# A hybrid encoder step: three PSUM banks for the scores instead of two, two for the dense products instead of three, and dense operands on multiples of 512 bytes

## The chip, the cores and the metric

One core of one Trainium2 chip runs the whole program. The metric is the device time of that core in microseconds (us). The kernel before took 2956.35 us, the median of three runs (2955.74 to 2959.2).

## The reference

One layer of a streaming encoder, on 2,128 token columns in one pass (64 of a running stream, 16 meta tokens, 2,048 of a new stream), model width 1,024:

```
h = rms_norm(x);  p = h @ w_in                       # 1024 -> attention, RG-LRU and GLA columns
o_att = rms_norm(softmax(q0 k0)v - lam*softmax(q1 k1)v)   # 4 heads, block-causal chunks of 64
o_lru = rg_lru(causal_dwconv(lx)) * gelu(lg)
o_gla = rms_norm(gla_blocked(gq, gk, gv, log_g)) * silu(gog)
x = x + concat(o_att, o_lru, o_gla) @ w_out
h = rms_norm(x)
x = x + (gelu(causal_dwconv3(h @ ffn_w_up)) * (h @ ffn_w_gate)) @ ffn_w_down   # 1024 -> 2816 -> 1024
y = rms_norm(x)
```

It also returns the new K and V rows and the end states of the recurrences and convolutions.

## The kernel before

**Precision.** Every dense product is three matmuls in fp32r: each operand is split into a high part and a rest (`whi`, `wlo` for weights; `hh`, `hl`, `h2h`, `h2l`, `gh`, `gl` for activations), and high x high, rest x high and high x rest are summed in one PSUM bank. A weight tile is 128 columns wide and is the stationary operand; the activations are the moving operand, up to 512 columns. So every matmul brings a weight load (the engine PEld) with it.

**Streams.** `Flow.run` takes steps in turn from three generators: `dense` (the input projection `win`, then the FFN of groups of tokens), `attention` (scores and values) and `recurrent` (RG-LRU and GLA). The order in which instructions stand on each engine is then made by the framework's scheduler from these streams' priorities and from the buffers that are free, so a different number of buffers gives another order everywhere.

**Stages.** The input projection (lines 641 and 643, tile `ps_w`) runs to some 800 us. Then come three groups of tokens, `FGROUPS = [[512], [512], [336, 256, 512]]`. For each, `wout` multiplies by w_out (L1434, tile `pd`), `up_gate` makes for each of 22 slices of the FFN one product `pu` and one `pg` per block of tokens (L1299, 24 matmuls each), and `down` adds them into the residual (L1366, tile `pd`, added to x by VectorE at L1372). Groups 1 and 2 run beside attention and recurrences, to about 2020 us. Group 3 (1,104 tokens) runs alone after it, with pools of its own opened in `open3`.

**Eviction.** A product leaves its bank in different ways. `pu` is copied out by ScalarE (L1316). `pg` is read by VectorE (L1334), and only after the convolution and GELU of `pu` (L1316 to L1329, ScalarE and VectorE in turn) are done. A score tile `ps_sc` (L1052, perhaps a mask at L1057, and L1059) is read twice: by VectorE for the row minimum `NB` (L1061) and then by ScalarE for the exponential `pc` (L1062).

**PSUM.** It has eight banks. Before: three for the dense products (`ps_w`, which up to 2020 us also serves `pd`), two for scores (`ps_s`), one each for transposes, values and recurrences. In group 3 the last five are given to `pd` (`ps_x`), while `pu` and `pg` keep `ps_w`.

**SBUF.** Pools are laid one behind the other from the left, and others from the right end. The small constants (`cst`) come first, then the weight buffers `wp` (two `raw`, three `whi`, three `wlo`, 4 KB per partition each), then the pools of the stage. From the tiles' sizes, the weight buffers began 32 bytes past a multiple of 512, and so did the activations of the projection and of groups 1 and 2. In group 3 the activations `h2h`, `h2l` began 480 bytes past one, and `gh`, `gl` (1,104 columns, with blocks at columns 0, 336 and 592) began at changing places.

Of the kernel before, what the change touches and what calls it, by code (L numbers as in the profile page):

```python
# [10 lines left out]
F32 = mybir.dt.float32  # L11
# [7 lines left out]
PSUM = bass.MemoryType.PSUM  # L19
DRAM = bass.MemoryType.DRAM  # L20

P = 128
# [41 lines left out]
FGROUPS = [[512], [512], [336, 256, 512]]  # L64
# [71 lines left out]
def tile_hymba_step(ctx, tc, xT, xkT, cache_v, wi, wo, wu, wg, wd, par, sgla, c_msk, yT_p, yT_s, nkT_p, nv_p, lh_p, lc_p, gs_p, fc_p,  # L136
                    nkT_s, nv_s, lh_s, lc_s, gs_s, fc_s):
    nc = tc.nc
# [20 lines left out]
    env = {}  # L159
# [12 lines left out]
    NPC, NRC, NW, NRAW, NSQ = 9, 9, 3, 2, 3  # L172
    cst = ctx.enter_context(tc.tile_pool(name="cst", bufs=1))
    wp = ctx.enter_context(tc.tile_pool(name="wp", bufs=1))
    ps_w = ctx.enter_context(tc.tile_pool(name="ps_w", bufs=3, space=PSUM))
    mstack = ExitStack()
    ps_s = mstack.enter_context(tc.tile_pool(name="ps_s", bufs=2, space=PSUM))
    ps_t = mstack.enter_context(tc.tile_pool(name="ps_t", bufs=1, space=PSUM))
    ps_o = mstack.enter_context(tc.tile_pool(name="ps_o", bufs=1, space=PSUM))
    ps_r = mstack.enter_context(tc.tile_pool(name="ps_r", bufs=1, space=PSUM))  # L180
# [17 lines left out]
    lrue = cst.tile([P, 16], F32, name="lrue")  # L198
    halo = cst.tile([P, NF, 2], F32, name="halo")
    fce = cst.tile([P, 2, 2, NF], F32, name="fce")  # L200

    def pr(name, i=0, n=1):
        a = PAR[name][0] + i
        return prm[:, a:a + n] if a < NPAR1 else prm2[:, a - NPAR1:a - NPAR1 + n]
# [70 lines left out]
    def w_take(key, n):  # L275
        while len(wq["ready"].get(key, ())) < n:
            w_split()
        return wq["ready"].pop(key)

    def w_used(n):  # L280
        wq["used"] += n
# [966 lines left out]
    p2 = ExitStack()  # L1248
# [9 lines left out]
    def open3():  # L1258
        env["hs"].close()
        env["dg"], env["rg"] = "dg", "rg"  # L1260
        env["ps"] = p2.enter_context(tc.tile_pool(name="ps_x", bufs=5, space=PSUM))

        env["hp"] = p2.enter_context(tc.tile_pool(name="hp3", bufs=1, side="right"))
        env["xp"] = [p2.enter_context(tc.tile_pool(name="xp3", bufs=4, side="right")),
                     p2.enter_context(tc.tile_pool(name="xp4", bufs=4))]
        env["ev"] = p2.enter_context(tc.tile_pool(name="ev3", bufs=2))
        env["gp"] = p2.enter_context(tc.tile_pool(name="gp3", bufs=5))

    x2 = {}
# [6 lines left out]
    def up_gate(g, ff, H, gt, norms):  # L1276
        (wu_,), (wg_,) = w_take(("up", g, ff), 1), w_take(("gate", g, ff), 1)
        ev2, gp = env["ev"], env["gp"]
        gw = sum(FGROUPS[g])
        gh = gp.tile([P, gw], F32R, tag="gh", name="gh")  # L1280
        gl = gp.tile([P, gw], F32R, tag="gl", name="gl")
        gt[ff] = (gh, gl)
        cw = [pr("fcw", 22 * w + ff) for w in range(3)]
        cb = pr("fcb", ff)
        goff = 0
        for bi, n in enumerate(FGROUPS[g]):
            yield from norms.pop(bi, ())
            us = []
            for a, b, kind in ffn_pieces(g, n):
                uh = ev2.tile([P, n + 2], F32, tag="uh", name="uh")  # L1290
                cc = ev2.tile([P, n], F32, tag="cc", name="cc")
                us.append((a, b, kind, uh, cc))

            def product(w_):
                ps = ps_w.tile([P, NMAX], F32, tag="w", name="pu" if w_ is wu_ else "pg")
                for k in range(KT):
                    hk, lk = H[bi][0][:, k], H[bi][1][:, k]
                    for i3, (wi_, hx) in enumerate(((0, hk), (0, lk), (1, hk))):
                        nc.tensor.matmul(ps[:, :n], lhsT=w_[wi_][:, k * P:(k + 1) * P], rhs=hx,  # L1299
                                         start=(k == 0 and i3 == 0), stop=(k == KT - 1 and i3 == 2))  # L1300
                    if k % 2 == 1:
                        w_pump()
                        yield 6 * n * 0.425
                        yield from beside(norms)
                env["prod"] = ps
            yield from product(wu_)
            pu = env["prod"]
            for a, b, kind, uh, cc in us:
                m = b - a
                if kind == "s":  # L1310
                    nc.gpsimd.tensor_copy(uh[:, 0:2], pr("fst", 0, 44).rearrange("p (w k) -> p k w", w=2)[:, ff, :])
                elif kind == "z":
                    nc.gpsimd.memset(uh[:, 0:2], 0.0)
                else:
                    nc.gpsimd.tensor_copy(uh[:, 0:2], halo[:, ff, :])
                nc.scalar.activation(out=uh[:, 2:2 + m], in_=pu[:, a:b], func=AF.Copy)  # L1316
                if kind == "s":
                    nc.gpsimd.tensor_copy(fce[:, 1, :, ff], uh[:, m:m + 2])
                else:
                    nc.gpsimd.tensor_copy(halo[:, ff, :], uh[:, m:m + 2])  # L1320
                nc.scalar.activation(out=cc[:, :m], in_=uh[:, 0:m], func=AF.Identity, scale=cw[0], bias=cb)  # L1321
                for w in (1, 2):
                    nc.vector.scalar_tensor_tensor(out=cc[:, :m], in0=uh[:, w:w + m], scalar=cw[w], in1=cc[:, :m],  # L1323
                                                   op0=ALU.mult, op1=ALU.add)

                nc.scalar.activation(out=uh[:, :m], in_=cc[:, :m], func=AF.Square, scale=GELU_A)
                nc.vector.scalar_tensor_tensor(out=uh[:, :m], in0=uh[:, :m], scalar=1.0, in1=cc[:, :m], op0=ALU.add,
                                               op1=ALU.mult)
                nc.scalar.activation(out=uh[:, :m], in_=uh[:, :m], func=AF.Tanh, scale=GELU_B)  # L1329
            yield from product(wg_)  # L1330
            pg = env["prod"]
            for a, b, kind, uh, cc in us:
                m = b - a
                nc.vector.scalar_tensor_tensor(out=cc[:, :m], in0=cc[:, :m], scalar=0.5, in1=pg[:, a:b], op0=ALU.mult,  # L1334
                                               op1=ALU.mult)
                nc.vector.scalar_tensor_tensor(out=cc[:, :m], in0=uh[:, :m], scalar=1.0, in1=cc[:, :m], op0=ALU.add,  # L1336
                                               op1=ALU.mult)
                gh_, gl_ = gh[:, goff + a:goff + b], gl[:, goff + a:goff + b]
                pool_scaled(gh_, cc[:, :m])
                minus(gl_, cc[:, :m], f(gh_))  # L1340
            goff += n
        w_used(2)

    def offsets(g):
        return [sum(FGROUPS[g][:b]) for b in range(len(FGROUPS[g]))]

    def down(g, q, gt, done=None, outs={}):
# [8 lines left out]
        for i, (ct, b) in enumerate(order):  # L1356
            half = ct // 4
            if half not in W:
                W[half] = w_take(("down", g, q, half), len(gts) // 2)
            o, n = offsets(g)[b], FGROUPS[g][b]  # L1360
            ps = env["ps"].tile([P, NMAX], F32, tag="w", name="pd")
            for j, (gh, gl) in enumerate(gts):
                c = j % 2 * NMAX + ct % 4 * P
# [14 lines left out]
    def beside(gens):  # L1378

        for g_ in list(gens.values()):  # L1380
            yield next(g_, 0)
# [253 lines left out]
```

## Time and profile before

| | |
|---|---|
| Median of three runs | 2956.35 us |
| Profiled execution: time, span | 2957.12 us, 2955.3 us |
| TensorE busy | 2841.2 us, 96% of the span, 16,031 matmuls |
| VectorE busy | 1890.9 us, 64% |
| ScalarE busy | 1138.1 us, 39% |
| GpSimd busy | 870.5 us, 29% |
| Mean granted TensorE clock | 0.982 of full |

The profiled execution took 1.8 us more than its span. Matmuls overlap in their records: one of 512 columns is listed with some 390 to 400 ns, while the next one starts 227 to 235 ns after it. So what a matmul costs is read from the distance of starts, and "busy" of TensorE holds small stalls that are not listed as idle time.

### The profile page before, as it was taken

To read this page: it belongs to the slowest core of one execution; us is meant where nothing else is said; L and a number is where in the kernel's file an instruction comes from. 1 tells how busy PE (TensorE), PEld (TensorE's weight loads), DVE (VectorE), ACT (ScalarE), POOL (GpSimd) and SP (SyncE) were. 2 spreads that over 40 slices of the span, in tenths; PEclk is the share of its full clock that TensorE was granted. 3 is DMA by queue.
4 is the path that set the end of the run, shared out by engine and by line. 5 is a ranking of instruction groups with operands and counts; after the bars stand their busy time and mean duration, and the time that the engine had idled before them with its cause. 6 is when DMAs were issued, how large, how long until landed. Compare 5 with 4: busy or idle time off the path is not lost.

```text
span 2955.3 us, 44538 instructions
## 1 busy us (share of the span) xinstructions
PE 2841.2 (96%) x16031; PEld 2508.7 (85%) x16031; DVE 1890.9 (64%) x3699; ACT 1138.1 (39%) x2589; POOL 870.5 (29%) x1212
## 2 busy tenths in 40 slices
PE   7999999999898998999999999999999999999997
PEld 7988899989876887787787888888989998999997
DVE  7677685778879879879969865333454333333335
ACT  5354554555555454545445433211222121212122
POOL 4435534434535445444424221000110000000001
PEclk9999999999999999999999999999999999999999
DMA  7675564656796776777875565685222222222222
GB/s 241 201 217 148 179 214 139 199 179 186 227 338 212 252 264 234 249 266 261 285 258 183 197 203 183 208 327 186 72 86 86 86 86 86 86 86 86 86 86 105
DMA packets 277930, 537.43 MB, mean 182 GB/s; under 512 B 31014, under 2 KB 170030, under 8 KB 277710
## 3 DMA queue, kind: packets, MB, share of 16 engines
q1 hardware_dynamic: 277566, 534.58, 54.9%
q8 instruction: 127, 2.08, 0.3%
q14 instruction: 93, 0.76, 0.1%
q10 hardware_dynamic: 144, 0.01, 0.0%
HBM read 382.74 MB, written 151.76 MB: 181 GB/s over the span
## 4 chain that ended last, share of the span: by engine, by line
PE 69%; DVE 14%; DMA 4%; issue 2%; ACT 2%; POOL 1%; SPq 0%; POOLq 0%; ACTq 0%; DVEq 0%
PE pd L1366 15%; PE pg L1299 14%; PE pu L1299 14%; PE pd L1434 6%; PE ps_w L641 5%; PE ps_w L643 3%; DVE pc L1100 3%; PE ps_o L1166 3%; PE ps_sc L1059 2%; PE ps_pt L1151 2%; PE ps_sc L1052 2%; DVE BD L886 1%; DVE NB L1061 1%; PE ps_r L891 1%; DVE y L435 1%
## 5 line engine op out<-in xcount | busy, mean ns | idle before, releaser
L257 POOL TENSOR_TENSOR wlo<-raw,whi 128x1024 fp32r<-128x1024 f32 (+1 forms) x104 | 249.8, 2404 | 309.6 <-ACT whi L151 278.5
L1062 ACT ACTIVATE pc<-ps_sc,NB 128x512 f32<-128x512 f32 (+6 forms) x400 | 224.5, 562 | 298.2 <-DVE NB L1061 262.6
L1299 PE MATMUL pu<-h2h,whi 128*128 128x512 f32 (+2 forms) x880 | 316.8, 360 | 5.0 <-ACT h2h L151 2.8
L1323 DVE SCALAR_TENSOR_TENSOR cc<-uh,prm,cc 128x512 f32<-128x512 f32 (+4 forms) x264 | 165.0, 634 | 242.9 <-ACT cc L1321 239.8
L1299 PE MATMUL pu<-h2l,whi 128*128 128x512 f32 (+2 forms) x880 | 316.2, 359 | 1.4 <-DVE h2l L157 1.4
L1299 PE MATMUL pu<-h2h,wlo 128*128 128x512 f32 (+2 forms) x880 | 316.5, 360 | 0.0
L1366 PE MATMUL pd<-gh,whi 128*128 128x512 f32 (+2 forms) x880 | 314.2, 360 | 2.1 <-DMA whi<-WS 1.4
L1299 PE MATMUL pg<-h2h,wlo 128*128 128x512 f32 (+2 forms) x880 | 315.6, 359 | 0.4 <-DMA wlo<-WS 0.4
L1299 PE MATMUL pg<-h2l,whi 128*128 128x512 f32 (+2 forms) x880 | 315.9, 359 | 0.0
L1299 PE MATMUL pg<-h2h,whi 128*128 128x512 f32 (+2 forms) x880 | 315.0, 358 | 0.7 <-DMA whi<-WS 0.5
L1366 PE MATMUL pd<-gh,wlo 128*128 128x512 f32 (+2 forms) x880 | 314.5, 358 | 0.0
L1366 PE MATMUL pd<-gl,whi 128*128 128x512 f32 (+2 forms) x880 | 312.9, 357 | 0.0
L1372 DVE TENSOR_TENSOR x<-x,pd 128x512 f32<-128x512 f32 (+2 forms) x240 | 141.8, 595 | 217.1 <-PE pd L1366 216.1
L641 PE MATMUL ps_w<-hh,whi 128*128 128x384 f32 (+2 forms) x768 | 259.1, 340 | 16.0 <-ACT whi L151 10.5
L1316 ACT ACTIVATE uh<-pu 128x336 f32<-128x336 f32 (+3 forms) x132 | 59.3, 464 | 539.6 <-PE pu L1299 539.1
L1061 DVE TENSOR_REDUCE NB<-ps_sc 128x1 f32<-128x512 f32 (+6 forms) x400 | 209.5, 529 | 86.8 <-PE ps_sc L1059 85.2
L641 PE MATMUL ps_w<-hl,whi 128*128 128x384 f32 (+2 forms) x768 | 259.6, 339 | 0.4 <-DVE hl L157 0.4
L641 PE MATMUL ps_w<-hh,wlo 128*128 128x384 f32 (+2 forms) x768 | 256.0, 335 | 0.3 <-DVE wlo L157 0.3
L154 POOL TENSOR_SCALAR gh<-cc 128x336 fp32r<-128x336 f32 (+3 forms) x132 | 72.9, 553 | 444.8 <-DVE cc L1336 440.0
L151 ACT ACTIVATE whi<-raw 128x1024 fp32r<-128x1024 f32 (+2 forms) x160 | 165.8, 1036 | 96.7 <-DMA raw<-in_wi 30.5
L1299 PEld LDWEIGHTS pu<-h2h,whi 128*128 128x128 f32 x880 | 167.4, 190 | 26.6 <-ACT h2h L151 3.2
L154 POOL TENSOR_SCALAR pc<-pc,fr 128x512 f32<-128x512 f32 (+4 forms) x200 | 156.8, 802 | 109.3 <-DVE fr L1082 86.1
(330 smaller groups left out, 7142.5 us busy)
## 6 DMA issues: line engine op xcount, KB each, us to landing
whi<-WS SPq DMA_DIRECT2D x148, 512.0 KB, 4.3
wlo<-WS SPq DMA_DIRECT2D x148, 512.0 KB, 4.3
raw<-in_wi SPq DMA_DIRECT2D x74, 512.0 KB, 4.1
WS<-whi SPq DMA_DIRECT2D x74, 512.0 KB, 3.1
WS<-wlo SPq DMA_DIRECT2D x74, 512.0 KB, 6.0
Kc<-KHL SPq DMA_DIRECT2D x48, 512.0 KB, 5.8
V<-VHL SPq DMA_DIRECT2D x48, 512.0 KB, 3.5
Q<-QHL SPq DMA_DIRECT2D x64, 256.0 KB, 4.4
```

The lines of the kernel that those rows point to most:

```text
L151: nc.scalar.activation(out=out, in_=in_, func=AF.Copy, scale=scale)
L154: nc.gpsimd.tensor_scalar(out, in_, s, 1.0, ALU.mult, ALU.mult)
L257: nc.gpsimd.tensor_tensor(out=lo[:, :n], in0=t[:, :n], in1=f(hi[:, :n]), op=ALU.subtract)
L641: nc.tensor.matmul(ps[:, :n], lhsT=wx, rhs=hx, start=st_, stop=sp_)
L643: nc.tensor.matmul(ps[:n, :wd_], lhsT=hx, rhs=wx, start=st_, stop=sp_)
L1061: nc.vector.tensor_reduce(NB[:qw, ti, m, ci:ci + 1], ps[:qw, :kt_], AX.X, ALU.min)
L1062: nc.scalar.activation(out=pv_[m][:qw, :kt_], in_=ps[:qw, :kt_], func=AF.Exp, scale=-1.0, bias=NB[:qw, ti, m, ci:ci + 1], accum_out=SS[:qw ...
L1299: nc.tensor.matmul(ps[:, :n], lhsT=w_[wi_][:, k * P:(k + 1) * P], rhs=hx, start=(k == 0 and i3 == 0), stop=(k == KT - 1 and i3 == 2))
L1323: nc.vector.scalar_tensor_tensor(out=cc[:, :m], in0=uh[:, w:w + m], scalar=cw[w], in1=cc[:, :m], op0=ALU.mult, op1=ALU.add)
L1366: nc.tensor.matmul(ps[:, :n], lhsT=w_, rhs=g_[:, o:o + n], start=(j == 0 and i3 == 0), stop=(j == len(gts) - 1 and i3 == 2))
L1372: nc.vector.tensor_tensor(x2[b, ct], x2[b, ct], ps[:, :n], ALU.add)
L1434: nc.tensor.matmul(ps[:, :n], lhsT=w_, rhs=g_, start=(k == 0 and i3 == 0), stop=(k == KT - 1 and i3 == 2))
```

## The change

Three things. The pool of the dense products gets two PSUM banks and the scores three; in group 3, `pd` gets six banks instead of five. A tile of 480 bytes that nothing reads (`pad0`) ends the constants, so that the weight buffers and all that lies behind them on the left begin at a multiple of 512 bytes. In group 3, two more such tiles (480 bytes on the right, 64 on the left) do the same for `h2h`, `h2l` and for `gh`, `gl`, and the three blocks inside `gh` and `gl` are laid out by size (512 at column 0, 336 at 512, 256 at 896, 1,152 columns in all), so that each begins at a multiple of 512 bytes. Each pad is written once by GpSimd.

```diff
-    ps_w = ctx.enter_context(tc.tile_pool(name="ps_w", bufs=3, space=PSUM))
+    ps_w = ctx.enter_context(tc.tile_pool(name="ps_w", bufs=2, space=PSUM))
     mstack = ExitStack()
-    ps_s = mstack.enter_context(tc.tile_pool(name="ps_s", bufs=2, space=PSUM))
+    ps_s = mstack.enter_context(tc.tile_pool(name="ps_s", bufs=3, space=PSUM))
...
     fce = cst.tile([P, 2, 2, NF], F32, name="fce")
+    nc.gpsimd.memset(cst.tile([P, 120], F32, name="pad0"), 0.0)
...
-        env["ps"] = p2.enter_context(tc.tile_pool(name="ps_x", bufs=5, space=PSUM))
-
+        env["ps"] = p2.enter_context(tc.tile_pool(name="ps_x", bufs=6, space=PSUM))
+
+        pad(p2.enter_context(tc.tile_pool(name="pad_r", bufs=1, side="right")), 480)
         env["hp"] = p2.enter_context(tc.tile_pool(name="hp3", bufs=1, side="right"))
...
         env["ev"] = p2.enter_context(tc.tile_pool(name="ev3", bufs=2))
+        pad(p2.enter_context(tc.tile_pool(name="pad_l", bufs=1)), 64)
         env["gp"] = p2.enter_context(tc.tile_pool(name="gp3", bufs=5))
...
-        gw = sum(FGROUPS[g])
+        at, gw = places(g)
...
-        goff = 0
         for bi, n in enumerate(FGROUPS[g]):
+            goff = at[bi]
...
-            goff += n
         w_used(2)
+
+    def places(g):
+
+        at, n = {}, 0
+        for b in sorted(range(len(FGROUPS[g])), key=lambda b: -FGROUPS[g][b]):
+            at[b] = n
+            n += -(-FGROUPS[g][b] // P) * P
+        return at, n
+
+    def pad(pool, n):
+        nc.gpsimd.memset(pool.tile([P, n // 4], F32, tag="pad", name="pad", bufs=1), 0.0)
...
-            o, n = offsets(g)[b], FGROUPS[g][b]
+            o, n = places(g)[0][b], FGROUPS[g][b]
```

The counts of instructions stay the same on every engine but GpSimd (three more); their order changes on all of them. Two places on TensorE show how. The first is in the stretch in which attention runs beside the first group of the FFN: score tiles of one head against one chunk of keys (`ps_sc`, `Kc`), the values of another head (`ps_o`), w_out (`pd`). Before:

```order
L1059 MATMUL ps_sc_12824<-Kc_12590,Q_12585 128x512
L1434 MATMUL pd_8990<-h2l0_8539,whi_8882 128x512
L722 MATMUL ps_r_13205<-xc_13036,prm2_167 128x256
L1166 MATMUL ps_o_12242<-ph_12371,V_12243 128x256 x2
L1166 MATMUL ps_o_12242<-pl_12372,V_12243 128x256
L1166 MATMUL ps_o_12242<-ph_12371,V_12243 128x256 x2
L1166 MATMUL ps_o_12242<-pl_12372,V_12243 128x256
L1166 MATMUL ps_o_12242<-ph_12408,V_12243 128x256 x2
L1166 MATMUL ps_o_12242<-pl_12409,V_12243 128x256
L1166 MATMUL ps_o_12242<-ph_12408,V_12243 128x256 x2
L1166 MATMUL ps_o_12242<-pl_12409,V_12243 128x256
L1052 MATMUL ps_sc_13078<-Kc_12592,Q_12585 128x512
```

The same score tiles in the changed kernel, where all numbers of tiles are two higher:

```order
L1053 MATMUL ps_sc_12826<-Kc_12592,Q_12587 128x512
L1060 MATMUL ps_sc_12826<-Kc_12592,Q_12587 128x512
L1053 MATMUL ps_sc_13080<-Kc_12594,Q_12587 128x512
L1060 MATMUL ps_sc_13080<-Kc_12594,Q_12587 128x512
L1053 MATMUL ps_sc_13099<-Kc_12594,Q_12587 128x512
L1060 MATMUL ps_sc_13099<-Kc_12594,Q_12587 128x512
L1191 MATMUL ps_on_12205<-dgt_12202,ones_164 128x256
L1053 MATMUL ps_sc_13120<-Kc_12594,Q_12587 128x512
```

Three score tiles now stand one behind the other, where ten other rows lay between the first and the second. Over the whole program the last score tile stood behind 6,220 of the 12,408 dense matmuls, and now stands behind 5,904.

The second place is in the input projection, near its start: `ps_w_580` and `ps_w_630` are two dense products that follow each other. Before:

```order
L641 MATMUL ps_w_535<-hh0_0_209,wlo_433 128x336
L641 MATMUL ps_w_580<-hh0_0_209,whi_470 128x336
L641 MATMUL ps_w_580<-hl0_0_210,whi_470 128x336
L641 MATMUL ps_w_630<-hh0_0_209,whi_548 128x336
L641 MATMUL ps_w_630<-hl0_0_210,whi_548 128x336
L641 MATMUL ps_w_580<-hh0_0_209,wlo_471 128x336
```

In the changed kernel the later one (now `ps_w_632`) begins behind the last matmul of the earlier (`ps_w_582`):

```order
L642 MATMUL ps_w_582<-hh0_0_211,whi_472 128x336
L642 MATMUL ps_w_582<-hl0_0_212,whi_472 128x336
L642 MATMUL ps_w_582<-hh0_0_211,wlo_473 128x336
L642 MATMUL ps_w_632<-hh0_0_211,whi_550 128x336
L642 MATMUL ps_w_632<-hl0_0_212,whi_550 128x336
L642 MATMUL ps_w_632<-hh0_0_211,wlo_551 128x336
```

With two banks a product has one other beside it: the one that waits to be read out, or the one that is filled next, not both.

## Rows read from the trace of the kernel before

**Rows 1.** Busy time of each engine in four stretches: from:to in us, length, then busy us and (count) of PE, PEld, DVE, ACT, POOL, then the granted TensorE clock, the DMA share and GB/s.

```profile
100.00:800.00 700.00, 666.80 (x4388) 629.35 (x4387) 526.55 (x1103) 355.76 (x900) 301.16 (x342) 0.99 0.62 185
800.00:1600.00 800.00, 758.26 (x3726) 621.54 (x3725) 679.12 (x1322) 411.07 (x956) 349.68 (x430) 0.96 0.77 257
1600.00:2020.00 420.00, 417.58 (x2031) 347.62 (x2030) 233.18 (x420) 126.69 (x276) 76.56 (x154) 1.00 0.65 225
...
2130.00:2940.00 810.00, 803.63 (x4762) 730.31 (x4760) 332.52 (x605) 167.06 (x308) 74.60 (x213) 1.00 0.24 84
```

**Rows 2.** Waits of TensorE between 100 and 2020 us: who waited, for whom, us in total, times, longest.

```profile
PE ps_sc L1052 <- ACT pc L1062: 22.4, 24, 3.5
PE ps_sc L1052 <- DMA Q<-QHL: 14.2, 7, 4.4
PE ps_o L1166 <- DVE pl L157: 8.2, 7, 2.2
...
PE pu L1299 <- DVE cc L1334: 2.2, 1, 2.2
```

**Rows 3.** The chain that ended last, in group 2 after attention is done: start us, us, what, count. Both pieces are whole products of 512 columns.

```profile
1908.21 5.44 PE pg L1299 x24
1913.65 5.44 PE pu L1299 x24
```

**Rows 4.** The same view in group 3: products of 512, 336 and 256 columns.

```profile
2390.20 5.60 PE pu L1299 x24
2395.81 5.60 PE pg L1299 x24
2401.41 3.72 PE pu L1299 x24
2405.12 3.71 PE pg L1299 x24
2408.83 2.83 PE pu L1299 x24
```

**Rows 5.** TensorE in order of time in the down product of group 3: start us, us, instruction. The first row is the first of twelve matmuls of 512 columns, the second is the one after the twelfth.

```profile
2513.65 0.40 PE L1366 MATMUL pd<-gh,whi 128*128 128x512 f32 x1
...
2516.43 0.32 PE L1366 MATMUL pd<-gh,whi 128*128 128x336 f32 x1
```

**Rows 6.** TensorE in order of time in w_out of group 3, 256 columns, the same operands' addresses as the last row of rows 4: the first of a product's 24 matmuls and the one after the 24th.

```profile
2038.90 0.28 PE L1434 MATMUL pd<-h2h,whi 128*128 128x256 f32 x1
...
2041.63 0.28 PE L1434 MATMUL pd<-h2h,whi 128*128 128x256 f32 x1
```

**Rows 7.** Groups by line and shape from 2130 us on: count (x), busy us, mean ns of one, idle time before them.

```profile
L1299 PE MATMUL pu<-h2h,whi 128*128 128x512 f32 x176 | 69.8, 397 | 2.8 <-ACT h2h L151 2.8
...
L1366 PE MATMUL pd<-gh,whi 128*128 128x512 f32 x176 | 69.0, 393 | 0.0
...
L1299 PE MATMUL pu<-h2h,whi 128*128 128x256 f32 x176 | 49.5, 281 | 0.0
```

**Rows 8.** TensorE in order of time in group 2: two pairs of score matmuls of 512 columns between two dense ones.

```profile
1670.90 0.40 PE L1052 MATMUL ps_sc<-Kc,Q 128*128 128x512 f32 x1
...
1671.83 0.39 PE L1299 MATMUL pu<-h2h,whi 128*128 128x512 f32 x1
```

**Rows 9.** TensorE in order of time: four transposes in fp32, each with a stationary tile of its own, and what follows.

```profile
1615.04 0.60 PE L1151 MATMUL ps_pt<-ident,pc 128*128 128x128 f32 x4
1615.47 0.51 PE L856 MATMUL ps_r<-prm,tl 128*128 128x4 f32 x4
```

**Rows 10.** TensorE in order of time in group 1, beside attention: the last matmul of a product `pg`, the first of the next `pu`, the first of the next `pg`.

```profile
1110.76 0.40 PE L1299 MATMUL pg<-h2h,wlo 128*128 128x512 f32 x1
1111.00 0.39 PE L1299 MATMUL pu<-h2h,whi 128*128 128x512 f32 x1
...
1117.82 0.39 PE L1299 MATMUL pg<-h2h,whi 128*128 128x512 f32 x1
```

**Rows 11.** VectorE in order of time: what stands before the reading of that first `pg`, and the reading (L1334).

```profile
1113.82 0.69 DVE L738 SCALAR_TENSOR_TENSOR tt<-tt,rc 128x512 f32<-128x512 f32 x1
1114.42 4.07 DVE L1323 SCALAR_TENSOR_TENSOR cc<-uh,prm,cc 128x64 f32<-128x64 f32 x2
1118.42 0.68 DVE L1061 TENSOR_REDUCE NB<-ps_sc 128x1 f32<-128x512 f32 x1
...
1120.29 0.74 DVE L1334 SCALAR_TENSOR_TENSOR cc<-cc,pg 128x64 f32<-128x64 f32 x2
```

**Rows 12.** VectorE in order of time in group 3: the readings of two products `pg`, the second and the fourth of rows 4.

```profile
2401.45 0.69 DVE L1334 SCALAR_TENSOR_TENSOR cc<-cc,pg 128x512 f32<-128x512 f32 x1 [1.07 <-PE pg L1299]
...
2408.87 0.50 DVE L1334 SCALAR_TENSOR_TENSOR cc<-cc,pg 128x336 f32<-128x336 f32 x1 [0.17 <-PE pg L1299]
```

**Rows 13.** Groups by line from 800 to 1600 us, columns as in rows 7.

```profile
L1052 PE MATMUL ps_sc<-Kc,Q 128*128 128x512 f32 (+4 forms) x189 | 77.9, 412 | 21.4 <-ACT pc L1062 16.7 <-DMA Q<-QHL 4.4
L1299 PE MATMUL pu<-h2h,whi 128*128 128x512 f32 x192 | 77.3, 404 | 2.3 <-DVE cc L1334 2.2
```

**Rows 14.** GpSimd in order of time: a write of a small constant tile.

```profile
2047.72 0.10 POOL L414 MEMSET r<- 128x4 f32 x1 [4.21 <-DMA out_y_prompt<-x]
```

**Rows 15.** TensorE in order of time: the first matmul of the last score tile of the program.

```profile
1813.13 0.31 PE L1052 MATMUL ps_sc<-Kc,Q 128*128 128x144 f32 x1
```

## Prediction

> **What bounds the kernel now.** I read the busy times by stretch first, since they say which engine is short of time and where [rows 1]. From 1600 us on TensorE is all there is: idle for 2.4 of 420 us and, in group 3, for 6.4 of 810 us, at the full granted clock. There the time is the number of matmuls times the distance of their starts. Between 100 and 1600 us TensorE still leads (758 of 800 us in the crowded half), but VectorE is at 679 of 800 us, 85%, TensorE is idle for 42 us, and the mean granted clock is 0.96: with levels of 2.4 and 1.2 GHz that is 8% of the stretch at the lower one.
>
> The waits of TensorE come next [rows 2]. The largest is that of a score tile for a bank that ScalarE still reads: 22.4 us in 24 waits. The scores' other wait, for their Q by DMA, is 14.2 us and is not touched. A dense product almost never waits for a bank: one wait of 2.2 us.
>
> Third, the price of a matmul, from the chain in order of time. A product of 24 matmuls of 512 columns takes 5.44 us in group 2 [rows 3], 226.7 ns each, and 5.60 us in group 3 [rows 4], 233.3 ns, with the same clock, engine and shape. 512 columns at 2.4 GHz are 213.3 ns, so 13.4 ns are lost in one place and 20 in the other. What differs is where the operands lie: in group 2 moving and stationary operand both begin 32 bytes past a multiple of 512, in group 3 the moving one 480 bytes past. In group 3's down product, whose blocks begin at changing places, twelve matmuls take 2.78 us, 231.7 ns each [rows 5]. Scores, with keys at 256 and queries at 480 bytes past, take 0.93 us for four, 232.5 ns [rows 8]. So the best speed seen is that of equal offsets, and no row shows an offset of 0.
>
> **The change, part by part.** The sum is made against the profiled execution, 2957.1 us, which is 0.8 above the median.
>
> *Offsets in group 3.* All operands of 512 columns get offset 0 on both sides. I take the speed of the rows with equal offsets. Up and gate: 22 slices x 2 products x 0.16 us = 7.0 us. w_out has 8 such products, 1.3 us. Down has 528 matmuls (three groups of 176 [rows 7]) x 5.0 ns = 2.6 us. Together -11 us, all of it on the path, since nothing else bounds group 3. The blocks of 256 columns I leave as they are: at one and the same pair of addresses they take 2.83 us per product [rows 4] and 2.73 us [rows 6], so the address alone doesn't decide there. The block of 336 keeps most of its offsets, as each of its eight slices is 1,344 bytes long.
>
> *Offsets elsewhere.* The projection and groups 1 and 2 go from 32 and 32 to 0 and 0. No row shows this, so I bound it. Downward: four fp32 transposes, each with new weights, start 107.5 ns apart [rows 9], 0.8 ns over two cycles for each of 128 columns. If all 12,408 dense matmuls lost only that, instead of 11 to 15 ns, about 12 ns each or 149 us would go. Upward: if offset 0 were as bad as group 3's places are now, groups 1 and 2 would lose 104 products x 0.16 us + 1,056 x 5.0 ns = 22 us. The nearest row is that of equal offsets, so I take 0.
>
> *The third bank for scores.* At best all of 22.4 us [rows 2]. 16.7 of them lie between 800 and 1600 us [rows 13], where VectorE has little time to spare: it must read each score tile (and ScalarE after it) at the same rate as before, and part of the wait comes back elsewhere. I take two thirds, -15 us, and 0 to -22 as bounds.
>
> *Two banks for dense products up to 2020 us.* This adds waits. 153 products of the projection and 200 of groups 1 and 2 go through these banks. If they waited as the 400 score tiles do now on two banks, 0.056 us each, that is 20 us. But a product fills its bank for 5.44 us and a score tile for 0.46, so the bank before it has far longer to be read: I take half, +10 us. Behind a waiting matmul stands all of TensorE's queue, scores and values too. The bounds are 0 and +77 (the slower rival below).
>
> *The new order.* The last score stands 316 dense matmuls earlier, 72 us at 227 ns each. That much work moves from a stretch with 5.2% idle time and clock 0.96 to one with 0.6% and 1.00 [rows 1]: 3.3 + 2.9 = -6 us. Bounds: 0 and twice that.
>
> *What costs nothing.* Two banks for `pu` and `pg` in group 3: `pg` is read within about 0.7 us of its last matmul [rows 12], while the product between it and the next user of its bank takes 2.8 to 5.6 us [rows 4]. If a reading came more than a product late there, each case would cost its excess. Six banks for `pd` in group 3: there is no wait for five [rows 7], so nothing to gain. The three pads are writes of about 0.1 us on GpSimd [rows 14], which is busy for 9% of group 3 and 43% before [rows 1]: hidden, 0.3 us if not.
>
> Sum: 2957.1 - 11 - 15 + 10 - 6 = 2935, less the 0.8: 2934 us.
>
> **The rivals.**
>
> *Alignment does nothing.* The difference between groups 2 and 3 could come from the order of shapes, since the 256-column blocks have two speeds at the same addresses [rows 4, 6]. Against it: the 512-column products hold 5.44 and 5.60 us each in its own group [rows 3, 4]. Then the 11 us stay: 2945 us. The Trainium skill speaks for this rival: "SBUF — State Buffer", section "Operand start alignment", asks only for starts on multiples of the element size and says that this is about legality, and the section "Specifications (TRN2)" gives access in lines of 16 bytes, of which 32 and 480 are both multiples. By that rule rows 3 and 4 should be equal, and they are not.
>
> *Offset 0 frees the array.* The 13 ns per matmul go wholly, as in the transposes. 6,504 dense matmuls stand behind the last score now, with nothing else to bound them: 78 us. Of the 5,904 ahead of it I count half, 35 us, the rest being taken by VectorE. 2934 + 11 - 113 = 2832 us. For it: the loss is there in every dense row, and no row has offset 0. Against it: scores with keys on a multiple of 256 are no faster than others [rows 8]. By "TensorE: Matmul & The Clock Gate", section "Back-to-back issue gap", of the Trainium skill, 512 columns would come every 215.8 ns (an estimate, from its formula for bf16); no dense row here comes near it.
>
> *The scores' wait only moves.* VectorE sets the pace from 100 to 1600 us, and the third bank makes TensorE wait for values or transposes instead. Terms of -15 and -6 go: 2955 us. For it: VectorE's 85%, and 8.2 us of waits of the values' matmuls for VectorE that stand there already [rows 2]. Against it: after 1600 us VectorE has time enough, and the new order puts more work there.
>
> *Slower: the gate product holds its bank.* The one place is the hand-over from `pg` to the next `pg` in groups 1 and 2 beside attention. A `pg` ends at about 1111 [rows 10], VectorE is held by other work for 4 us in the convolution alone, and reads it only at 1120.29 to 1121.03 [rows 11]. With three banks the next `pg` began at 1117.82; with two it would have waited 3.2 us. There are 24 such pairs between 800 and 1600 us (192 / 8 [rows 13]): 77 us if all lose that, and 2934 - 10 + 77 = 3001 us. From 10 of 24 on (32 us) it eats the whole gain. Against it: the scheduler knew of two banks when it made the order. In the Trainium skill, "A second HAM failure mode: psum-queue depth-cycling" (same page) tells of short stalls between banks that also cost clock; the 0.96 in rows 1 is in the stretch with most waits, which agrees.
>
> **How the numbers follow.** Chances: forecast 0.40 (2934, its own range 2920 to 2948), alignment nothing 0.17 (2945), wait only moves 0.15 (2955), offset 0 frees the array 0.10 (2832), slower 0.18 (3001, from 2963 up). A measurement of this kernel tells 0.2% or 6 us from no change: 2950.4 and 2962.3 are the borders. Faster: 0.40 + 0.12 of the second + 0.03 of the third + 0.10 = 0.65. Same: 0.05 + 0.09 = 0.14. Slower: 0.18 + 0.03 = 0.21. The range of 2885 to 2990 leaves out the free array and the worse part of the slower case, some 0.17.
>
> **What would show it.** Right: products of 512 columns at 5.44 us in group 3, those of group 2 unchanged; the scores' wait for ScalarE below 8 us; waits of `pu`, `pg`, `pd` and `ps_w` for ScalarE and VectorE near 10 us; the last score some 30 us or more ahead of its 1813 us [rows 15]. Wrong: 5.60 us still, or much less than 5.44 in any group; or waits for dense banks of 30 us and more, with a lower clock between 800 and 1600 us.

## The result and the profile after

The changed kernel takes 2988.84 us (median of four runs, 2984.45 to 2994.22), beside 2957.77 us (2955.74 to 2960.65) for the kernel before. The ratio is 1.0105, with a 95% interval of 1.0083 to 1.0127: 31 us slower, where some 23 us faster was forecast. The profiled execution took 2984.45 us, the shortest of the four.

The page of the changed kernel, its first lines; before, TensorE was busy for 2841.2 of 2955.3 us:

```profile
span 2982.7 us, 44559 instructions
...
PE 2842.8 (95%) x16031; PEld 2514.3 (84%) x16031; DVE 1883.1 (63%) x3699; ACT 1136.2 (38%) x2589; POOL 871.9 (29%) x1215
```

TensorE has as much to do as before (1.6 us more), but its idle time went from 114.1 to 139.9 us: 25.8 of the 27.4 us by which the span grew. Where it sits idle is read from the stretches of [rows 1], columns as there:

```profile
100.00:800.00 700.00, 664.24 (x4333) 628.03 (x4332) 527.92 (x1121) 352.87 (x903) 299.17 (x346) 0.98 0.61 181
800.00:1600.00 800.00, 751.87 (x3784) 617.02 (x3782) 673.98 (x1317) 417.00 (x970) 350.00 (x428) 0.97 0.79 260
1600.00:2020.00 420.00, 408.56 (x1936) 337.77 (x1936) 220.78 (x394) 116.93 (x253) 79.02 (x148) 0.98 0.59 210
2130.00:2940.00 810.00, 805.70 (x4800) 739.18 (x4799) 330.56 (x601) 167.54 (x310) 74.45 (x213) 1.00 0.25 86
```

TensorE's busy time fell in every stretch up to 2020 us (by 2.6, 6.4 and 9.0 us), and the stretch from 1600 us on, which had been full, now has 11.4 us of idle time. Group 3 looks the opposite: 2.1 us more busy and 38 matmuls more in the same 810 us, though these hold work from some 32 us earlier in the program. The chain of waits puts a date on the border. Its longest piece in w_out of group 3, first of the kernel before and then of the changed one (start us, us, what, count):

```profile
2036.13 75.97 PE pd L1434 x463
```

```profile
2068.61 75.74 PE pd L1447 x463
```

Up to that point 32.5 us were lost. From it to the end of the span, 919.2 us became 914.1: 5.1 us were won.

The waits of TensorE from 0 to 2020 us answer to [rows 2] (those begin at 100 us):

```profile
PE ps_sc L1053 <- DMA Q<-QHL: 14.0, 9, 4.1
PE ps_o L1167 <- ACT ph L151: 8.8, 6, 3.4
PE ps_sc L1053 <- ACT pc L1063: 8.4, 10, 1.7
PE ps_on L1191 <- POOL dgt L154: 7.6, 6, 2.7
...
PE ps_r L806 <- ACT tt L724: 7.0, 2, 3.9
...
PE ps_r L892 <- DVE att L896: 6.1, 3, 4.5
PE pd L1379 <- DVE x L1385: 5.5, 3, 4.6
PE pg L1302 <- DVE cc L1337: 5.5, 3, 3.0
PE ps_o L1167 <- DVE pl L157: 5.0, 6, 1.8
...
PE ps_r L723 <- ACT tt L724: 2.4, 2, 2.2
```

The scores' wait for a bank fell from 22.4 to 8.4 us, as forecast. The waits of dense products for a bank (those of `ps_w`, `pu`, `pg` and `pd` for `x`, `cc`, `e_q`, `e_lgt`, `e_k` and `e_gv`, which read the product before; summed over the whole list) rose from 9.2 to 20.1 us, as forecast too. What was not forecast is the rest: the waits of values, recurrences, norms and transposes (`ps_o`, `ps_on`, `ps_r`, `ps_pt`, `ps_nb`, `ps_sq`, `ps_lam`) rose from 31.7 to 52.5 us. Some of these are waits for data: `ps_o` multiplies the `ph` that it waits for. Others are waits for a bank of which the stream has but one, before as after: `tt` and `att` read the product in `ps_r` before the next can begin, and the waits for these two rose from 1.4 to 15.5 us. In the kernel before they were:

```profile
PE ps_r L805 <- ACT tt L723: 1.0, 2, 0.7
...
PE ps_r L891 <- DVE att L895: 0.4, 1, 0.4
```

The last score tile now begins at 1766.76 us, 46.4 us earlier than in [rows 15]:

```profile
1766.76 0.23 PE L1053 MATMUL ps_sc<-Kc,Q 128*128 128x144 f32 x1
```

In group 3 the products answer to [rows 4]:

```profile
2412.21 3.71 PE pg L1302 x24
2415.92 2.87 PE pu L1302 x24
2418.79 2.88 PE pg L1302 x24
2421.67 5.47 PE pu L1302 x24
2427.14 5.44 PE pg L1302 x24
```

Products of 512 columns went from 5.60 to 5.44 and 5.47 us, those of 336 stayed, those of 256 went from 2.83 to 2.87. In group 2 a product of 512 columns takes what it took in [rows 3]:

```profile
1863.85 5.44 PE pu L1302 x24
1869.29 5.44 PE pg L1302 x24
```

### The profile page after: what moved, and what is told of

Same layout as the page of the kernel before. It is cut to its first block, busy times and chain, and to the rows that moved or that the text cites. A ratio compares the mean times of both kernels' runs of the same rounds, so it can differ in the third digit from the quotient of the medians.

```text
span 2982.7 us, 44559 instructions
## 1 busy us (share of the span) xinstructions
PE 2842.8 (95%) x16031; PEld 2514.3 (84%) x16031; DVE 1883.1 (63%) x3699; ACT 1136.2 (38%) x2589; POOL 871.9 (29%) x1215
## 4 chain that ended last, share of the span: by engine, by line
PE 47%; DVE 5%; issue 2%; DMA 1%; POOL 1%; ACT 1%; SPq 0%; POOLq 0%; DVEq 0%; ACTq 0%
PE pd L1379 14%; PE pg L1302 13%; PE pu L1302 13%; PE pd L1447 3%; PE ps_o L1167 1%; DVE pc L1101 1%; PE ps_pt L1152 1%; PE ps_sc L1053 1%; DVE y L436 1%; PE ps_sc L1060 1%; DVE NB L1062 1%; DMA whi<-WS 1%; POOL pc L154 0%; DVE cc L1326 0%; DVE pl L157 0%
## 5 line engine op out<-in xcount | busy, mean ns | idle before, releaser
L154 POOL TENSOR_SCALAR pc<-pc,fr 128x512 f32<-128x512 f32 (+4 forms) x200 | 163.3, 834 | 130.5 <-DVE fr L1083 112.0
L1379 PEld LDWEIGHTS pd<-gh,whi 128*128 128x128 f32 x880 | 166.0, 189 | 35.6 <-DVE x L1385 7.6
```

Of the source, the lines that this page charges most:

```text
L154: nc.gpsimd.tensor_scalar(out, in_, s, 1.0, ALU.mult, ALU.mult)
L1379: nc.tensor.matmul(ps[:, :n], lhsT=w_, rhs=g_[:, o:o + n], start=(j == 0 and i3 == 0), stop=(j == len(gts) - 1 and i3 == 2))
```

## The experiments

Offsets and banks come apart cleanly: in the traces the offsets leave the order of all matmuls as it was, and the banks alone give the changed kernel's order.

**The offsets alone, and the banks alone.** The first is the changed kernel with

```diff
-    ps_w = ctx.enter_context(tc.tile_pool(name="ps_w", bufs=2, space=PSUM))
+    ps_w = ctx.enter_context(tc.tile_pool(name="ps_w", bufs=3, space=PSUM))
...
-    ps_s = mstack.enter_context(tc.tile_pool(name="ps_s", bufs=3, space=PSUM))
+    ps_s = mstack.enter_context(tc.tile_pool(name="ps_s", bufs=2, space=PSUM))
...
-        env["ps"] = p2.enter_context(tc.tile_pool(name="ps_x", bufs=6, space=PSUM))
+        env["ps"] = p2.enter_context(tc.tile_pool(name="ps_x", bufs=5, space=PSUM))
```

and the second is the kernel before with the same three lines the other way round. Expected of the first:

> The offsets alone: three dense banks and two score banks as before (five for pd in group 3), all pads and the new layout of gh and gl. The order of instructions on every engine is that of the kernel before, but for the pads' writes. Theory A (offsets only help in group 3, the banks lose the rest): the 512-column products of group 3 take 5.44 to 5.47 us, those of 256 columns 2.87, and the time is the one before less the 5 us that group 3 lost in the changed kernel: 2952, 2948 to 2956. Theory B (offset 0 in the projection and in groups 1 and 2 is what costs the time): 2980 or more, with the start of group 3 about 30 us later than before.

Of the second:

> The banks alone: two dense, three for scores, six for pd in group 3; no pads, old layout. The order is that of the changed kernel. Theory A: all of the loss and none of the gain, 2988.8 + 5 = 2994 us, 2990 to 2998, group 3 starting near 2069 us as in the changed kernel. Theory B: near 2957.

Measured: 2950.25 us, ratio to the kernel before on the same chip 0.9988 (0.9975 to 1.0000), and 2992.51 us, 1.0140 (1.0120 to 1.0160). The banks lose it all, and the offsets give back about 5 us, at the edge of what can be told. Offset 0 in the projection and in groups 1 and 2 neither helps nor harms.

**What of an offset counts.** The pads of group 3 and the new layout without `pad0`, banks as before:

```diff
-    nc.gpsimd.memset(cst.tile([P, 120], F32, name="pad0"), 0.0)
```

> Offsets in group 3 alone, banks as before, no pad at the constants: the weights stay 32 bytes past a multiple of 512. h2h and h2l of group 3 start on a multiple of 512 (480 past before), gh and gl 32 past, like the weights. If the distance between moving and stationary operand (modulo 512) decides: up and gate of 512 columns stay near 5.60 us, the down product drops to 227 ns per matmul; the time falls by some 2 us. If a start of the moving operand on a multiple of 512 decides: up and gate drop to 5.44 to 5.47 us, down stays at 231 ns; the time falls by some 5 us.

Measured: 2954.13 us, 1.0005 (0.9987 to 1.0022). The time can't tell 2 us, but the rows can. The chain in group 3 (products of 256, 512 and 336 columns), where h2h and h2l start on a multiple of 512 and the weights 32 bytes past one:

```profile
2389.01 2.84 PE pg L1301 x24
...
2397.45 5.60 PE pg L1301 x24
2403.05 3.70 PE pu L1301 x24
```

TensorE in order of time in a down product, where gh, gl and the weights all start 32 bytes past: the first of twelve matmuls of 512 columns, and the one behind the twelfth:

```profile
2509.24 0.39 PE L1378 MATMUL pd<-gh,whi 128*128 128x512 f32 x1
...
2511.95 0.31 PE L1378 MATMUL pd<-gh,whi 128*128 128x336 f32 x1
```

5.60 us as before, although the moving operand lies on a multiple of 512; and 2.71 us for twelve, 225.8 ns each, where [rows 5] had 231.7, although nothing lies on one. So the distance of the two operands decides, not the multiple.

**Two dense and two score banks.** One line, one bank unused:

```diff
-    ps_w = ctx.enter_context(tc.tile_pool(name="ps_w", bufs=3, space=PSUM))
+    ps_w = ctx.enter_context(tc.tile_pool(name="ps_w", bufs=2, space=PSUM))
```

> Two dense banks and two score banks up to group 3, one bank unused; no pads. Only the third dense bank is gone against the kernel before. Theory D (the missing dense bank makes the loss, by waits for banks and by the order that it forces): 2985 to 3010, at least as slow as the banks alone. Theory N (the third score bank makes the loss, since scores run ahead and their softmax delays the other streams' work): 2957 + 12 for waits of dense banks = 2969, 2960 to 2975, with the waits of values and recurrences for ScalarE, VectorE and GpSimd as low as in the kernel before (ps_o for ph 3 us, ps_on 2, ps_r for tt 1).

Measured: 2987.60 us, 1.0126 (1.0102 to 1.0149). Theory N falls: the missing dense bank makes the loss, with the score banks untouched. The third score bank on top of it gains nothing (1.0140 with it; the intervals overlap). The waits of TensorE from 0 to 2020 us in two and two, for the scores' banks, and the longest for a dense one:

```profile
PE ps_sc L1052 <- ACT pc L1062: 9.7, 13, 1.8
...
PE ps_w L643 <- DVE e_lgt L515: 4.9, 2, 4.1
```

The scores' wait for a bank is 9.7 us here, with two banks, where the kernel before had 22.4 and the changed one 8.4. So the new order took most of it away, and not the third bank.

**Where it arises.** The dense pool was split into two, one that is closed at the end of the projection and one that is opened at the first w_out, with two banks in one and three in the other (the pools of the other streams went to the right end of PSUM for it):

```diff
...
     p1 = ExitStack()
+    ps_w = p1.enter_context(tc.tile_pool(name="ps_w", bufs=2, space=PSUM))
...
     def open2():
-        env["ps"] = ps_w
+        nonlocal ps_w
+        env["ps"] = ps_w = p2.enter_context(tc.tile_pool(name="ps_v", bufs=3, space=PSUM))
```

> Two dense banks during the input projection alone (a pool of its own, closed at its end), three from the first w_out on, two score banks, no pads. With three banks in both pools the order of the kernel before comes out on every engine. Theory P (the loss arises in the projection, whose products are read out by chains of several instructions on ScalarE and VectorE): 2985, 2978 to 2992, first w_out 15 us or more later than 817. Theory F (it arises beside attention, where a gate product holds its bank until the convolution is done): 2957, 2950 to 2964.

With three in the first and two in the second:

> Three dense banks during the projection, two from the first w_out to the end, two score banks, no pads. Theory P: 2957, 2950 to 2964. Theory F: 2980 or more, with waits of pu, pg and pd for cc and x of 15 us or more up to 2020 us. Both in part: each of the two runs near 2971.

Measured: 2973.59 us, 1.0069 (1.0046 to 1.0092), and 2974.73 us, 1.0061 (1.0039 to 1.0083). It is both in part: 16 and 17 us, together about the 32 of two and two. So neither the projection's chains of read-outs nor the gate product alone is the culprit.

**Another order under the same banks.** Only the weight of one stream was changed, under the banks of before and under those after:

```diff
-    flow.run((dense(), 1875e3, 0), (attention(), 560e3, 30000),
+    flow.run((dense(), 1880e3, 0), (attention(), 560e3, 30000),
```

> Nothing of the change: banks and offsets as before, but the weight of the dense stream is 1880e3 instead of 1875e3, which by the scheduler gives another order (some 1,600 of 14,792 rows on TensorE stand elsewhere). If only the number of banks matters: 2957, 2951 to 2963. If one order among others is worth as much as the change lost (lottery): off by 10 us or more, to either side.

> The changed kernel's banks without pads as in the run of the banks alone, with the weight of the dense stream at 1880e3: another order under the same banks. If the number of banks makes the loss: 2992, 2984 to 3000. If the order was a bad draw: off by 10 us or more from the 2992.5 of the banks alone.

Measured: 2964.35 us, 1.0027 (1.0011 to 1.0043), and 2980.81 us, 1.0086 (1.0063 to 1.0109). An order is a draw worth some 10 us: the first is 7 us worse than the order before, the second 12 us better than that of the banks alone. The order that the changed kernel got was not a good one, but the better one still loses 23 us.

**Reading dense products out first.** The instructions that read a dense product were put ahead of attention's in the scheduler, here for `pd` (likewise around the puts of the projection and around the chains behind `pu` and `pg`):

```diff
+            tc.cur_priority -= 40000
             nc.vector.tensor_tensor(x2[b, ct], x2[b, ct], ps[:, :n], ALU.add)
+            tc.cur_priority += 40000
```

> The banks of the changed kernel (two dense, three for scores, no pads), and the instructions that read a dense product out (the puts of the projection, the chain behind pu and pg, the addition of pd to x) get 40,000 more priority in the scheduler, more than attention's 30,000. Theory H (a full dense bank that is read late leaves TensorE without a filler, so that each late softmax, transpose or norm shows as idle time): shorter waits of full banks, some half of the 35 us back, 2975, 2965 to 2982. Theory L (any new order is a new draw, and read-out time doesn't matter): 2980 to 2995 like the two orders run so far.

> The kernel before (three dense banks, two for scores, no pads) with the same priority for the read-out of dense products. Theory H: with three banks the filler is there in most cases: 2957, 2948 to 2962. Theory L: a draw between 2950 and 2970. In both theories scores and values come later, since their softmax stands behind the read-outs; if that costs more than banks do, 2970 or more.

Measured: 3006.41 us, 1.0171 (1.0141 to 1.0201), and 2954.91 us, 0.9996 (0.9983 to 1.0008). Theory H falls. The waits of dense products for banks did get shorter, from some 22 us with the banks alone to some 14, but the time did not: with two dense banks the median is 14 us longer still (the intervals of the ratios, 1.0141 to 1.0201 and 1.0120 to 1.0160, overlap). The scores' wait for a bank rose meanwhile from 8.1 to 15.0 us, since their softmax stands behind the read-outs. With three dense banks the waits for them went from 9.2 to 3.6 us, without any change of the time.

**The order of two banks, with three banks to run in.** The names of all instructions in the order made for two and two were written into the kernel before, and neighbours on each engine tied to each other:

```diff
+        for a, b in zip(row, row[1:]):
+            tc.add_manual_dep(b, a.name, mybir.DependencyInfo(mybir.DependencyClass.NoSync, mybir.DependencyReason.DATA), reason="pin")
```

> The banks and offsets of the kernel before (three dense, two for scores), but the order of instructions on all engines is held to that which the scheduler made for two dense and two score banks (edges without waits between neighbours on each engine). Theory O (the order that two banks force makes the loss): 2988, 2980 to 2996, like the run of two and two. Theory W (the waits for banks at run time make it): 2957, 2950 to 2965. Between them, the distance from either end says how much each has.

Measured: 2984.38 us, 1.0093 (1.0076 to 1.0110). This is the run that decides. Its trace has the 16,031 matmuls in the order of two and two, and by the medians 29 of the 32 us are lost with all three banks there; by the ratios it is 0.0093 of 0.0126, some three quarters. The stretches up to 2020 us of two and two:

```profile
0.00:400.00 400.00, 355.01 (x2197) 335.53 (x2198) 292.65 (x638) 200.04 (x493) 176.74 (x201) 0.96 0.66 194
...
sum 2020.00, PE 1910.79 PEld 1656.09 DVE 1499.07 ACT 943.95 POOL 779.77; mean PE 477.70 PEld 414.02 DVE 374.77 ACT 235.99 POOL 194.94
```

and of its order with three banks:

```profile
0.00:400.00 400.00, 353.70 (x2161) 334.09 (x2162) 289.34 (x632) 196.51 (x486) 174.83 (x198) 0.94 0.65 192
...
sum 2020.00, PE 1910.80 PEld 1655.98 DVE 1497.53 ACT 942.87 POOL 779.79; mean PE 477.70 PEld 414.00 DVE 374.38 ACT 235.72 POOL 194.95
```

TensorE is busy for 1910.8 us in both, and was for 1925.6 in the kernel before:

```profile
sum 2020.00, PE 1925.63 PEld 1677.97 DVE 1509.36 ACT 945.59 POOL 778.25; mean PE 481.41 PEld 419.49 DVE 377.34 ACT 236.40 POOL 194.56
```

The waits of dense products for banks come to 11.4 us in two and two; with the third bank there, not one is left in the list, and the idle time stays. What fills it are waits of the other streams (100 to 2020 us):

```profile
PE ps_sc L1052 <- DMA Q<-QHL: 15.6, 6, 4.5
PE ps_o L1166 <- DVE pl L157: 12.8, 12, 3.1
PE ps_sc L1052 <- ACT pc L1062: 11.3, 14, 1.8
PE ps_pt L1151 <- DVE pl L157: 7.8, 9, 4.5
PE ps_o L1166 <- ACT ph L151: 7.5, 8, 2.8
```

`ps_o` for `pl`, `ps_pt` for `pl` and `ps_o` for `ph` were 8.2, 3.2 and 3.0 us before, `ps_sc` for `pc` 22.4. `ps_o` waits for data there, and `ps_pt` for the one bank of the transposes, which `pl` still reads. Whether a second bank for transposes or recurrences would have helped was not run.

**Is it the balance of the streams?** In each of the orders that two dense banks gave, fewer dense matmuls stood ahead of the last score tile than before. So that count was moved by attention's weight alone, with the banks of before (640e3 and 480e3 for 560e3), and moved back up under two dense banks (wholly, with 360e3 for two and two; in good part, with 440e3 for two and three):

```diff
-    flow.run((dense(), 1875e3, 0), (attention(), 560e3, 30000),
+    flow.run((dense(), 1875e3, 0), (attention(), 640e3, 30000),
```

> Banks and offsets as before, but the weight of the attention stream is 640e3 instead of 560e3, so that attention runs ahead as it does with two dense banks: 6,109 dense matmuls stand ahead of the last score tile (6,220 before, 6,070 with two banks from w_out on, 5,973 with two and two). Theory B (how much dense work stands beside attention decides, and the banks act through that): 2957 + 111 x 0.1 = 2968, 2963 to 2978. Theory M (two banks force a finer misplacement that this count only goes along with): 2957, 2950 to 2964.

> The same with 480e3: 6,399 dense matmuls ahead of the last score tile. Theory B: 2957 - 179 x 0.1 = 2939, 2930 to 2950. Theory M: 2957, 2950 to 2966.

> Two dense and two score banks as in the run of two and two, but the weight of the attention stream is 360e3 instead of 560e3, so that 6,222 dense matmuls stand ahead of the last score tile, as many as in the kernel before (6,220; 5,973 with 560e3). Theory B (the count decides): back to 2957, 2950 to 2966. Theory M (two banks force a worse order at any balance): 2980 or more. Half way, near 2972: both.

> The banks of the changed kernel (two dense, three for scores, no pads) with 440e3 for attention: 6,121 dense matmuls ahead of the last score tile instead of 5,904. Theory B: 2992.5 - 217 x 0.1 = 2971, 2962 to 2978. Theory M: 2985 or more.

Measured in this order: 2982.22 us, 1.0089 (1.0076 to 1.0102); 2963.94 us, 1.0020 (1.0006 to 1.0035); 2975.55 us, 1.0072 (1.0055 to 1.0089); 2992.43 us, 1.0138 (1.0122 to 1.0155). Theory B has the right direction in the first, but not the size: 26 us, where it said 11 and at most 21. Attention running ahead costs that even with three banks, so a loss of this size doesn't need a missing bank. But more dense work beside attention gained nothing, restoring the count under two and two brought back a part (9 of 32 us by the medians; 1.0126 to 1.0072), and moving it up under two and three nothing. The balance is a part of it at most. What else in an order for two banks makes the other streams wait longer was not found.

One rival stays open. The weights of the streams may simply suit the order of before: of the four other orders run with three dense banks throughout, none was faster clear of noise (from 1 us less to 26 us more), and the six with two banks throughout lost 23 to 51 us. No search for good weights under two banks was run, so how much of the loss they would give back is not known.

**The version that beats both.** The offsets alone, with the 256-column block left as far from the weights as it was (448 bytes), by pads around h2h1 and h2l1 and by its place in gh and gl:

```diff
+            if len(widths) > 1 and n == 256:
+                pad(pool, 448, "pa")
...
+        if len(at) > 1:
+            at[1], n = at[1] + 112, n + 128
```

> The run of the offsets alone, but the block of 256 columns in group 3 (h2h, h2l, gh, gl) begins 448 bytes past a multiple of 512 while the weights lie on one, as far apart as in the kernel before; 512 columns stay at equal offsets. If the distance helps or hurts by width: products of 256 columns of up and gate at 2.83 us instead of 2.87, those of 512 stay at 5.44 to 5.47; 44 x 0.045 + some 1 us in down and w_out = 3 us less than the offsets alone: 2947, 0.997 of the kernel before. If the 256 blocks are slower for another reason, 2950.

Measured: 2944.29 us, 0.9965 (0.9952 to 0.9978), faster than the kernel before by some 10 us. Its chain in group 3:

```profile
2399.66 2.83 PE pg L1308 x24
2402.49 5.44 PE pu L1308 x24
2407.93 5.44 PE pg L1308 x24
2413.37 3.71 PE pu L1308 x24
```

The 256-column products are back at 2.83 us, while 512 columns keep 5.44. From the piece of 463 matmuls in w_out (at 2028.84 us) to the end of its span of 2937.0 us it takes 908.2 us: 11.0 less than the kernel before.

## Why the prediction was wrong

The measured 2988.84 us lies just inside the stated range, but by luck: the upper end was set for the slower rival, whose mechanism did not come true (below).

**The step that failed** is "the new order". It said that 316 dense matmuls, 72 us, move out of the poorer stretch into the better one, for -6 us with bounds of 0 and -12. They did move, but the last score tile came only 46 us earlier, not 72: the stretch ahead of it lost 26 us for what it still held. The step took the share of idle time of a stretch as given, whatever stands in it, and its bounds left out a loss. The run with the pinned order gives the term its size, for the order of two and two: +29 us by the medians instead of -6. That alone makes the forecast 2934 + 35 = 2969 us. With all four terms as measured (offsets -5, third score bank 0, waits for dense banks +3, order +29) the sum is 2957 + 27 = 2984 us, 5 us short of the median of 2988.84. The changed kernel's own order was not pinned; the banks alone, which have it, took 5 us more than two and two. Why these orders lose is not shown. That less dense work is left to cover the waits for softmax, norms and recurrences fits the lists of waits; the runs on the balance show that a mere count of it does not explain the loss.

**Dense banks at run time (+10).** The prediction counted one wait of 2.2 us for a dense bank before; with those of `ps_w` and `pd` it was 9.2. The waits rose by 10.9 us (9.2 to 20.1), the size forecast. What they are worth as time is not settled: with the order held, taking all 11.4 us of two and two away moved the median by 3 us (2987.60 to 2984.38) and the ratio by 0.0033 or 10 us (1.0126 to 1.0093), and the intervals of the ratios just overlap. The term may have been right.

**The third score bank (-15).** The wait fell by 14.0 us, but 12.7 of these had gone in two and two already, with two banks for scores, and the third bank did not shorten the time there. The term took a wait of one order for a price of the bank; the new order left little of that wait to save. The rival "the scores' wait only moves" is right in that nothing was gained, and waits of values, recurrences and norms did grow; that the third bank moved them is not shown, since the order had changed too.

**Offsets in group 3 (-11).** Right in mechanism, and half in size: 5.1 us of the changed kernel. The 512-column products did as said (5.44 to 5.47). "The blocks of 256 columns I leave as they are" was wrong: they got 0.04 to 0.05 us slower per product, 44 of them 2 us. With their old distance kept, group 3 wins 11.0 us. That this is the forecast number is partly luck: in the down product of that version matmuls of 256 columns start 114 ns apart, and they did so 118 ns apart before (medians), which was not in the sum. The prediction argued from two speeds at one pair of addresses [rows 4, 6] that the address doesn't decide there. Those two speeds stay unexplained, but the address has its part, with the opposite sign.

**Offsets elsewhere (0) and what was costed at nothing** held: the offsets alone show no change outside group 3, and with two banks in group 3 `pu` and `pg` wait 1.5 us for ScalarE.

**The other rivals.** "Alignment does nothing" is refuted by 5.44 us. The rule that stood beside it, from the Trainium skill ("SBUF — State Buffer", section "Operand start alignment"), asks only for a multiple of the element size and says that it is about legality; the rows differ between offsets that are all legal, so it does not speak of this speed. "Offset 0 frees the array" fell: 5.44 us in group 2, as before. The slower rival had nearly the right time (from 2963 up) by a wrong mechanism: `pg` waited for `cc` three times, 5.5 us in all, not 77. The rule beside it, "A second HAM failure mode: psum-queue depth-cycling" in "TensorE: Matmul & The Clock Gate" of the Trainium skill, says that short stalls between groups of matmuls on cycling banks make the clock swing; from 800 to 1600 us the granted clock was 0.97 after and 0.96 before, so no run here shows that the missing bank cost clock there. In the stretches beside it the clock did fall (0.99 to 0.98, and 1.00 to 0.98), and over the whole span from 0.982 to 0.977. What that cost was not taken apart, but two and two lost its 32 us at 0.981.

## What to carry to other kernels

Where a scheduler makes the order, a bank is first of all an input to the scheduler: price its loss by the order that it makes too, not only by the waits for it that the trace shows, and hold the order fixed to tell the two apart. A wait that the trace lists belongs to one order as well: the scores' wait went with the order, before a bank was added for it. A stretch's share of idle time is no property of the place: the stretch ahead of the last score tile lost 26 us here when the order changed and dense work left it. And a change made of parts that don't touch each other's order (offsets, banks) is best tried part by part: the offsets, once the block of 256 columns kept its distance, were worth 10 us by themselves.

## What the runs showed that was not expected

The speed of an fp32r matmul went with the distance between the starts of its moving and stationary operands (taken modulo 512 bytes, since the weights pass through buffers of 4 KB without a change of speed), and the sign depended on the width. At 512 columns equal starts gave 5.44 us per 24 matmuls (226.7 ns each; `pu` in group 3 at most 5.47) and distances of 448 and 480 bytes 5.60 (233.3 ns), whether the moving operand lay on a multiple of 512 or not. At 256 columns equal starts gave 2.87 us (119.6 ns) and a distance of 448 bytes 2.83 (117.9 ns) in up and gate and 2.73 in [rows 6], one of 480 bytes 2.84. Other distances were not run, and why the distance counts is open. Products of 336 columns, whose eight slices start at changing distances in every version, took 3.69 to 3.72 us throughout.
